# Tree attention on one core: loads in groups of four heads by first use, transposes behind the values and two pairs ahead

## The chip, the cores and the metric

The kernel runs on one core of one Trainium2 chip. The metric is device time in microseconds for one execution. The core's engines are TensorE (PE in the profile, with its weight loads as PEld), VectorE (DVE), ScalarE (ACT), GpSimd (POOL) and SyncE (SP), and 16 DMA engines move data.

## What is computed

Attention for 8 batches of 12 heads, with 512 positions of 64 elements each, in float32. The positions are the nodes of a binary tree, and each attends to itself and to its ancestors alone.

```python
    scale = 1.0 / np.sqrt(dim)
    mask = np.zeros((seq, seq))
    for i in range(seq):
        mask[i, i] = 1
        parent = i
        while parent > 0:
            parent = (parent - 1) // 2
            mask[i, parent] = 1

    scores = np.einsum('bhqd,bhkd->bhqk', Q, K) * scale
    scores = scores + (1 - mask) * (-1e9)
    weights = np.exp(scores - np.max(scores, axis=-1, keepdims=True))
    weights = weights / (np.sum(weights, axis=-1, keepdims=True) + 1e-10)
    return np.einsum('bhqk,bhkd->bhqd', weights, V).astype(np.float32)
```

## The kernel before

**Units.** The work unit is a pair of heads: 8 batches of 6 pairs, 48 pairs, numbered 0 to 47. A head's 512 positions lie as 128 partitions of 4 positions each. The mask is not added as numbers: two small constant matrices of codes (`ctile`) multiplied with each other give a large negative number where a query must not see a key, and TensorE accumulates q times k onto it in PSUM. Because each node has few ancestors, only two strips of scores are made, `st` (one key tile for all queries) and `stx` (for each of four groups of queries its own key tile), instead of the full 512 by 512.

**Loads.** `load` (L216) issues DMAs from GpSimd that read float32 from HBM and write bf16 tiles `qs`, `ks`, `vs`, one tile per batch and kind, six buffers of each. The list `plan` (L200) holds (iteration from which it may be issued, tensor, batch, first head, last head), and it is worked off in its written order: in batches 1 to 6 mostly Q and K of heads 0 to 5, V of the next batch, then Q and K of heads 6 to 11. Nothing but `load` runs on GpSimd. A load waits for the load eight before it, whose semaphore it takes over.

**A pair's steps.**
- `transposes(i)`: TensorE turns q and k of two heads by 16 matmuls into the PSUM tiles `tq` and `tk`; VectorE copies `tq` to `qt` (L297), ScalarE copies `tk` to `kt` (L298). q and k must have landed.
- `scores(i)`: into `st` two mask matmuls and two of q and k, then ScalarE's exponential to `et` (L324); into `stx` two mask matmuls and eight of q and k, then the exponential to `etx` (L335).
- `values(i)`: 24 matmuls of `et` and `etx` with V in the layouts `v1` and `vx`, whose last column of ones gives the sum of the weights, into the PSUM tile `o`; VectorE takes the reciprocal of the sums (`rec`, L364) and multiplies (`of`, L367); SyncE issues the output DMA (L371).
- `spread(b)` makes the layouts `v1` and `vx` of a batch from `vs`, as ten copies on VectorE (L261), three buffers of each layout.

Each of the PSUM tiles `tq`, `tk`, `st`, `stx`, `o` has one buffer.

**Order.** TensorE, VectorE, ScalarE and GpSimd each execute in the written order. The prologue is `load(3)`, `transposes(0)`, `scores(0)`, `transposes(1)`, the spread of six heads of batch 0, `transposes(2)`. Then iteration i issues:

```python
            load(i + 9)
            if i + 1 < N:
                scores(i + 1)
            if i + 3 < N:
                transposes(i + 3)
            values(i)
```

and after it one or two copies of the next batch's spread. So q and k of a pair are transposed two iterations before the iteration whose scores read them.

Of the kernel before, what the change touches and what calls it, by code (L numbers as in the profile page):

```python
# [126 lines left out]
def kernel(  # L127
# [8 lines left out]
    B, H, S, D = Q.shape  # L136
# [3 lines left out]
    HP = H // 2  # L140
# [11 lines left out]
    for t in range(T):  # L152
        o = sorted(range(T), key=lambda r: KCOL[t, r])
        at = [KCOL[t, r] for r in o]
# [32 lines left out]
    for i in range(NV):  # L187
# [10 lines left out]


    plan = [(0, Q, 0, 0, 2), (0, K, 0, 0, 2), (0, V, 0, 0, 6), (0, Q, 0, 2, 6),  # L200
            (0, K, 0, 2, 6), (0, V, 0, 6, H), (0, Q, 0, 6, H), (0, K, 0, 6, H),
            (3, Q, 1, 0, 6), (3, K, 1, 0, 6), (3, V, 1, 0, H), (6, Q, 1, 6, H),
            (6, K, 1, 6, H), (6, V, 2, 0, H)]
    for b in range(2, B):
        at = HP * b - 3
        plan += [(at, Q, b, 0, 6), (at, K, b, 0, 6)]
        if b < B - 1:
            plan += [(at + 2, V, b + 1, 0, H), (at + 3, Q, b, 6, H),
                     (at + 3, K, b, 6, H)]
        else:  # L210
            plan += [(at + 3, Q, b, 6, 10), (at + 3, K, b, 6, 10),
                     (at + 5, Q, b, 10, H), (at + 5, K, b, 10, H)]
    plan.reverse()
    loaded = {}
# [1 line left out]
    def load(upto):  # L216
        while plan and plan[-1][0] <= upto:
            _, src, b, h0, h1 = plan.pop()
            kind = "q" if src is Q else "k" if src is K else "v"
            if (kind, b) not in loaded:  # L220
                loaded[kind, b] = stage.tile([P, H, T * D], bf16, name=kind + "s")
            nc.gpsimd.dma_start(  # L222
                out=loaded[kind, b][:, h0:h1, :],
                in_=src[b, h0:h1].rearrange("h (p t) d -> p h (t d)", t=T),
            )
# [33 lines left out]
    def copies(ops):  # L259
        for o, i in ops:  # L260
            nc.vector.tensor_copy(out=o, in_=i)  # L261

    pairs = [(b, hp) for b in range(B) for hp in range(HP)]
    N = len(pairs)
    state = {}

    def transposes(i):
        b, hp = pairs[i]
        qs, ks = loaded["q", b], loaded["k", b]
        tq = psumT.tile([P, 512], bf16)  # L270
        tk = psumT.tile([P, 576], bf16)

        def put(o, src, t, mat):
            for hi in range(2):
                nc.tensor.matmul(  # L275
                    out=o[D * hi:D * hi + D], rhs=perms[mat],
                    lhsT=src[:, 2 * hp + hi, D * t:D * t + D],
                    start=True, stop=True, is_transpose=True,
                )

        put(tq[:, 64:192], qs, 0, 1)
        put(tq[:, 0:384].rearrange("d (c x) -> d c x", c=2)[:, :, 0:64], qs, 1, 0)
        for t in range(2, T):
            put(tq[:, P * t:P * t + P], qs, t, 0)
        for t in range(T):
            at = kput[t][1]
            if at[1] - at[0] == 32:
                step, run = at[2] - at[0], 64
            else:
                step, run = at[1] - at[0], 32  # L290
                assert at[2] - at[1] == step
            o = tk[:, at[0]:]
            o = bass.AP(o.tensor, o.offset, [list(o.ap[0]), [step, P // run], [1, run]])
            put(o, ks, t, 2 + t)
        qt = work.tile([P, 512], bf16)
        kt = work.tile([P, 512], bf16)
        nc.vector.tensor_copy(out=qt[:, :], in_=tq[:, :])  # L297
        nc.scalar.copy(  # L298
            out=kt[:, :].rearrange("d (i j x) -> d i j x", j=2, x=32),
            in_=tk[:, :].rearrange("d (j i x) -> d i j x", j=2, x=32)[:, 0:8],  # L300
        )
        state[i] = (qt, kt)

    def scores(i):
        b, hp = pairs[i]
        q_, k_ = state[i]
        st1 = psumS.tile([P, 2, 512], fp32)
        stx = psumS.tile([P, 2, 512], fp32)

        def mm(dst, lhsT, rhs, first):  # L310
            nc.tensor.matmul(  # L311
                out=dst, lhsT=lhsT, rhs=rhs, start=first, stop=True,
                skip_group_check=not first,
            )

        hb = [slice(D * hi, D * hi + D) for hi in range(2)]
        q = [q_[hb[hi], :] for hi in range(2)]
        k = [k_[hb[hi], :] for hi in range(2)]
        for hi in range(2):
            mm(st1[:, hi, :], ck1[hb[hi], :], cq1[hb[hi], :], True)  # L320
        for hi in range(2):
            mm(st1[:, hi, :], k[hi][:, 32 * K1:32 * K1 + P], q[hi], False)
        et1 = et1pool.tile([P, 2, 512], bf16)
        nc.scalar.activation(  # L324
            out=et1[:, :, :], in_=st1[:, :, :], func=AF.Exp, scale=scale
        )
        for hi in range(2):
            mm(stx[:, hi, 0:384], ckx[hb[hi], :], cqx[hb[hi], :], True)
        for c in range(T):
            for hi in range(2):  # L330
                mm(stx[:, hi, 96 * c:96 * c + 96],
                   k[hi][:, 32 * XW[c]:32 * XW[c] + P],
                   q[hi][:, P * c + 32:P * c + P], False)
        etx = etxs[i % NX]
        nc.scalar.activation(  # L335
            out=etx[:, :, :, 32:P],
            in_=stx[:, :, 0:384].rearrange("p h (c q) -> p h c q", c=T),
            func=AF.Exp, scale=scale,
        )
        state[i] = (et1, etx)  # L340

    def values(i):
        b, hp = pairs[i]
        v1, vx = v1s[b % NV], vxs[b % NV]
        et1, etx = state.pop(i)
        o2 = psumO.tile([P, 2, 512], fp32)
        for hi, order in ((0, (0, 1)), (1, (0, 1)), (0, (2, 3)), (1, (2, 3))):
            h = 2 * hp + hi
            for t in order:
                for kind in range(2):  # L350
                    parts = ((0, P, t),) if t >= 2 else (
                        (0, 64, 1 - t), (64, P, t))
                    for p0, p1, c in parts:
                        if kind == 0:
                            e, v = et1[:, hi, P * c + p0:P * c + p1], v1[:, h, 0:D + 1]
                        else:
                            e, v = etx[:, hi, c, p0:p1], vx[:, h, c, 0:D + 1]
                        nc.tensor.matmul(  # L358
                            out=o2[p0:p1, hi, (D + 1) * t:(D + 1) * (t + 1)],
                            lhsT=e, rhs=v, start=kind == 0, stop=kind == 1,  # L360
                        )
        o4 = o2[:, :, 0:T * (D + 1)].rearrange("p h (t x) -> p h t x", t=T)
        rec = opool.tile([P, 2, T, 1], fp32)
        nc.vector.reciprocal(out=rec[:, :, :, :], in_=o4[:, :, :, D:D + 1])  # L364
        of = opool.tile([P, 2, T * D], fp32)
        of4 = of[:, :, :].rearrange("p h (t d) -> p h t d", t=T)
        nc.vector.tensor_tensor(  # L367
            out=of4, in0=o4[:, :, :, 0:D],
            in1=rec[:, :, :, :].to_broadcast([P, 2, T, D]), op=ALU.mult,
        )  # L370
        nc.sync.dma_start(  # L371
            out=out[b, 2 * hp:2 * hp + 2].rearrange(
                "h (p t) d -> p h (t d)", t=T
            ),
            in_=of[:, :, :],
        )

    E = mybir.EngineType
    with tc.manual_schedule(engines={E.PE, E.DVE, E.Activation, E.Pool}):
        load(3)  # L380
        transposes(0)
        scores(0)
        transposes(1)
        copies(spread(0, 0, 6))
        transposes(2)
        for i in range(N):
            b, hp = pairs[i]
            load(i + 9)
            if i + 1 < N:
                scores(i + 1)  # L390
            if i + 3 < N:
                transposes(i + 3)
            values(i)
            if b == 0:
                if hp in (0, 3):
                    todo = spread(0, 6, H) if hp == 0 else spread(1, 0, H)
                cuts = (0, 3, 6, 10)
                copies(todo[cuts[hp % 3]:cuts[hp % 3 + 1]])
            elif b + 1 < B:
                if hp == 0:  # L400
                    todo = spread(b + 1, 0, H)
                cuts = (0, 1, 3, 5, 6, 8, 10)
                copies(todo[cuts[hp]:cuts[hp + 1]])


# [28 lines left out]
```

## Time and profile before

| | us |
|---|---|
| median of 13 executions | 158.77 (157.67 to 161.07) |
| the profiled execution, device time | 161.07 |
| its span, first to last instruction | 159.0 |
| TensorE matmuls busy | 116.8 (73%) |
| ScalarE busy | 105.8 (67%) |
| VectorE busy | 103.4 (65%) |
| GpSimd busy | 38.5 (24%) |
| load queue (q0), share of 16 DMA engines | 87.8% |
| output queue (q1), share of 16 DMA engines | 28.6% |
| mean granted TensorE clock | 0.931 |

The span is what the profile covers; the device time of the same execution has about 2 us more around it. The shares of the two DMA queues are the times that their packets took, and packets of both queues overlap on an engine, so their sum can pass 100%. TensorE's clock is granted in stretches: it is 1.00 or 0.50 of full speed. Busy shares are means over the whole span; the span has a long stretch in which the DMA engines are full and a shorter one at the end in which they are not.

### The profile page before, as it was taken

To read this page: it belongs to the slowest core of one execution; us is meant where nothing else is said; L and a number is where in the kernel's file an instruction comes from. 1 tells how busy PE (TensorE), PEld (TensorE's weight loads), DVE (VectorE), ACT (ScalarE), POOL (GpSimd) and SP (SyncE) were. 2 spreads that over 40 slices of the span, in tenths; PEclk is the share of its full clock that TensorE was granted. 3 is DMA by queue.
4 is the path that set the end of the run, shared out by engine and by line. 5 is a ranking of instruction groups with operands and counts; after the bars stand their busy time and mean duration, and the time that the engine had idled before them with its cause. 6 is when DMAs were issued, how large, how long until landed. Compare 5 with 4: busy or idle time off the path is not lost.

```text
span 159.0 us, 5902 instructions
## 1 busy us (share of the span) xinstructions
PE 116.8 (73%) x2592; PEld 85.4 (54%) x2592; DVE 103.4 (65%) x243; ACT 105.8 (67%) x145; POOL 38.5 (24%) x49
## 2 busy tenths in 40 slices
PE   0437599683999169995999189987977179998960
PEld 0215377462767047773777157756754058776740
DVE  2107567898999315994799437995979125996541
ACT  3142467685899317995699448986978117998950
POOL 7955441331321224222222224221301000000000
PEclk9999999999999957999599969999999956999998
DMA  5999999999999999999999999999999998442342
GB/s 140 147 181 197 197 199 220 222 232 233 220 235 236 239 221 199 229 235 244 221 229 236 243 221 220 221 241 236 226 237 233 241 197 157 139 138 95 122 154 99
DMA packets 50953, 32.32 MB, mean 203 GB/s; under 512 B 1520, under 2 KB 50800, under 8 KB 50928
## 3 DMA queue, kind: packets, MB, share of 16 engines
q0 software_dynamic: 37584, 18.88, 87.8%
q1 hardware_dynamic: 13344, 13.08, 28.6%
q8 instruction: 20, 0.33, 0.8%
q14 instruction: 5, 0.04, 0.1%
HBM read 38.24 MB, written 12.58 MB: 320 GB/s over the span
## 4 chain that ended last, share of the span: by engine, by line
DMA 76%; PE 8%; DVE 5%; issue 3%; POOL 3%; ACT 2%; ACTq 0%; POOLq 0%
DMA qs<-in_Q_dram 40%; DMA ks<-in_K_dram 36%; PE o L358 3%; DVE of L367 2%; PE st L311 2%; ACT etx L335 2%; PE stx L311 1%; DVE vx L261 1%; POOL vs L222 1%; POOL qs L222 1%; PE tk L275 1%; POOL ks L222 1%; PE tq L275 1%; DVE rec L364 1%; ACT et L324 1%
## 5 line engine op out<-in xcount | busy, mean ns | idle before, releaser
L324 ACT ACTIVATE et<-st 128x1024 bf16<-128x1024 f32 x48 | 50.5, 1053 | 19.6 <-PE st L311 19.5
L298 ACT COPY kt<-tk 128x512 bf16<-128x512 bf16 x48 | 29.6, 616 | 26.7 <-PE tk L275 26.7
L358 PE MATMUL o<-v,et 128*64 128x65 bf16 (+1 forms) x576 | 38.9, 204 | 6.6 <-DVE v L261 4.0
L335 ACT ACTIVATE etx<-stx 128x768 bf16<-128x768 f32 x48 | 40.1, 836 | 0.4 <-PE stx L311 0.4
L358 PE MATMUL o<-vx,etx 128*64 128x65 bf16 (+1 forms) x576 | 38.6, 202 | 0.0
L358 PEld LDWEIGHTS <-et 128*64 128x64 bf16 (+1 forms) x576 | 31.0, 113 | 9.0 <-DVE v L261 4.5
L367 DVE TENSOR_TENSOR of<-o,rec 128x512 f32<-128x512 f32 x48 | 33.2, 691 | 1.8 <-DVE rec L364 0.2
L275 PE MATMUL tq<-ptile,qs 128*64 128x128 bf16 x384 | 21.9, 242 | 14.9 <-DMA qs<-in_Q_dram 13.3
L275 PE MATMUL tk<-ptile,ks 128*64 128x128 bf16 x384 | 21.6, 241 | 14.9 <-DMA ks<-in_K_dram 14.6
L297 DVE COPY qt<-tq 128x512 bf16<-128x512 bf16 x48 | 20.2, 422 | 18.2 <-PE tq L275 17.2
L358 PEld LDWEIGHTS <-etx 128*64 128x64 bf16 (+1 forms) x576 | 30.9, 114 | 1.2 <-issue 1.2
L261 DVE COPY vx<-vs 32x1536 bf16<-32x1536 bf16 (+3 forms) x54 | 28.4, 526 | 1.5
L364 DVE RECIPROCAL rec<-o 128x8 f32<-128x8 f32 x48 | 9.7, 202 | 29.4 <-PE o L358 29.2
L311 PEld LDWEIGHTS <-kt 64*128 64x128 bf16 x480 | 20.4, 100 | 9.2 <-issue 4.6
L275 PEld LDWEIGHTS <-ks 128*64 128x64 bf16 x384 | 15.4, 123 | 16.5 <-DMA ks<-in_K_dram 16.2
L275 PEld LDWEIGHTS <-qs 128*64 128x64 bf16 x384 | 13.9, 118 | 19.0 <-DMA qs<-in_Q_dram 14.7
L222 POOL DMA_DIRECT2D qs<-in_Q_dram x18 | 15.1, 841 | 35.0 <-DMA qs<-in_Q_dram 10.5
L222 POOL DMA_DIRECT2D ks<-in_K_dram x18 | 14.7, 819 | 31.6 <-DMA vs<-in_V_dram 10.2
L311 PE MATMUL st<-qt,kt 64*128 64x512 bf16 x96 | 20.4, 413 | 0.2
L311 PE MATMUL st<-ctile 64*128 64x512 bf16 x96 | 20.4, 420 | 0.0
L311 PEld LDWEIGHTS <-ctile 64*128 64x128 bf16 x192 | 12.2, 97 | 14.1 <-issue 5.1
L311 PE MATMUL stx<-qt,kt 64*128 64x96 bf16 x384 | 18.4, 213 | 1.0 <-issue 1.0
(11 smaller groups left out, 42.8 us busy)
## 6 DMA issues: line engine op xcount, KB each, us to landing
out_dram<-of SPq DMA_DIRECT2D x48, 256.0 KB, 6.3
qs<-in_Q_dram POOLq DMA_DIRECT2D x14, 384.0 KB, 27.5
ks<-in_K_dram POOLq DMA_DIRECT2D x14, 384.0 KB, 26.4
vs<-in_V_dram POOLq DMA_DIRECT2D x7, 768.0 KB, 27.2
vs<-in_V_dram POOLq DMA_DIRECT2D x2, 384.0 KB, 9.0
qs<-in_Q_dram POOLq DMA_DIRECT2D x2, 256.0 KB, 16.6
ks<-in_K_dram POOLq DMA_DIRECT2D x2, 256.0 KB, 16.0
ctile<-tree_codes SPq DMA_DIRECT2D x1, 288.0 KB, 2.8
```

The costliest lines, as they stand in the source:

```text
L222: nc.gpsimd.dma_start(out=loaded[kind, b][:, h0:h1, :], in_=src[b, h0:h1].rearrange("h (p t) d -> p h (t d)", t=T),)
L261: nc.vector.tensor_copy(out=o, in_=i)
L275: nc.tensor.matmul(out=o[D * hi:D * hi + D], rhs=perms[mat], lhsT=src[:, 2 * hp + hi, D * t:D * t + D], start=True, stop=True, is_transpos ...
L297: nc.vector.tensor_copy(out=qt[:, :], in_=tq[:, :])
L298: nc.scalar.copy(out=kt[:, :].rearrange("d (i j x) -> d i j x", j=2, x=32), in_=tk[:, :].rearrange("d (j i x) -> d i j x", j=2, x=32)[:, 0:8],
L311: nc.tensor.matmul(out=dst, lhsT=lhsT, rhs=rhs, start=first, stop=True, skip_group_check=not first,)
L324: nc.scalar.activation(out=et1[:, :, :], in_=st1[:, :, :], func=AF.Exp, scale=scale)
L335: nc.scalar.activation(out=etx[:, :, :, 32:P], in_=stx[:, :, 0:384].rearrange("p h (c q) -> p h c q", c=T), func=AF.Exp, scale=scale,)
L358: nc.tensor.matmul(out=o2[p0:p1, hi, (D + 1) * t:(D + 1) * (t + 1)], lhsT=e, rhs=v, start=kind == 0, stop=kind == 1,)
L364: nc.vector.reciprocal(out=rec[:, :, :, :], in_=o4[:, :, :, D:D + 1])
L367: nc.vector.tensor_tensor(out=of4, in0=o4[:, :, :, 0:D], in1=rec[:, :, :, :].to_broadcast([P, 2, T, D]), op=ALU.mult,)
```

## The change

It has three parts.

1. The load plan. From batch 1 on, Q and K come in three groups of four heads instead of two of six, each group placed in the order in which its pairs are used, with V of the next batch between the second and the third group; batch 0 is split in the same manner. There are 61 load instructions instead of 45, for the same bytes.
2. The iteration's order on TensorE. It was scores(i+1), transposes(i+3), values(i). It becomes scores(i+1), values(i), transposes(i+2), and `transposes(2)` leaves the prologue. On VectorE the copy `qt` therefore stands behind `rec` and `of` of the iteration instead of ahead of them.
3. The spread copies of the next batch. In batches 1 to 6 they start with the second pair of the batch instead of the first, and come two at a time.

```diff
     plan = [(0, Q, 0, 0, 2), (0, K, 0, 0, 2), (0, V, 0, 0, 6), (0, Q, 0, 2, 6),
-            (0, K, 0, 2, 6), (0, V, 0, 6, H), (0, Q, 0, 6, H), (0, K, 0, 6, H),
-            (3, Q, 1, 0, 6), (3, K, 1, 0, 6), (3, V, 1, 0, H), (6, Q, 1, 6, H),
-            (6, K, 1, 6, H), (6, V, 2, 0, H)]
-    for b in range(2, B):
-        at = HP * b - 3
-        plan += [(at, Q, b, 0, 6), (at, K, b, 0, 6)]
+            (0, K, 0, 2, 6), (0, V, 0, 6, H), (1, Q, 0, 6, 10), (1, K, 0, 6, 10),
+            (3, Q, 0, 10, H), (3, K, 0, 10, H), (3, V, 1, 0, H)]
+    for b in range(1, B):
+        at = HP * b - 2
+        plan += [(at, Q, b, 0, 4), (at, K, b, 0, 4),
+                 (at + 2, Q, b, 4, 8), (at + 2, K, b, 4, 8)]
         if b < B - 1:
-            plan += [(at + 2, V, b + 1, 0, H), (at + 3, Q, b, 6, H),
-                     (at + 3, K, b, 6, H)]
+            plan += [(at + 3, V, b + 1, 0, H), (at + 4, Q, b, 8, H),
+                     (at + 4, K, b, 8, H)]
         else:
-            plan += [(at + 3, Q, b, 6, 10), (at + 3, K, b, 6, 10),
+            plan += [(at + 4, Q, b, 8, 10), (at + 4, K, b, 8, 10),
                      (at + 5, Q, b, 10, H), (at + 5, K, b, 10, H)]
...
         copies(spread(0, 0, 6))
-        transposes(2)
         for i in range(N):
             b, hp = pairs[i]
             load(i + 9)
             if i + 1 < N:
                 scores(i + 1)
-            if i + 3 < N:
-                transposes(i + 3)
             values(i)
+            if i + 2 < N:
+                transposes(i + 2)
             if b == 0:
                 if hp in (0, 3):
                     todo = spread(0, 6, H) if hp == 0 else spread(1, 0, H)
                 cuts = (0, 3, 6, 10)
                 copies(todo[cuts[hp % 3]:cuts[hp % 3 + 1]])
-            elif b + 1 < B:
-                if hp == 0:
+            elif b + 1 < B and hp:
+                if hp == 1:
                     todo = spread(b + 1, 0, H)
-                cuts = (0, 1, 3, 5, 6, 8, 10)
-                copies(todo[cuts[hp]:cuts[hp + 1]])
+                copies(todo[2 * hp - 2:2 * hp])
```

## The prediction

> **What bounds the kernel now.** I read the page first, for the share of each resource; then the chain of waits, for what ended last; then the timeline of one pair of heads without a stall, for durations and latencies.
>
> ```profile
> span 159.0 us, 5902 instructions
> ...
> DMA  5999999999999999999999999999999998442342
> ...
> DMA 76%; PE 8%; DVE 5%; issue 3%; POOL 3%; ACT 2%; ACTq 0%; POOLq 0%
> ```
>
> Each digit of the DMA row is 4 us. The 16 DMA engines are full up to about 133 us and a third busy in the last 26. So there are two stages: one in which transfers set the pace, and a tail in which compute works off what is left. The chain shows where one becomes the other:
>
> ```profile
> 97.11 31.09 DMA ks<-in_K_dram
> 128.20 0.04 issue
> 128.25 0.64 PE tk L275 x8
> ...
> 154.91 0.69 DVE of L367
> ```
>
> At 128.2 TensorE gets the second half of K of batch 6, for the transposes of pair 39. The values of pair 36 stand behind them, so pairs 36 to 47, twelve of 48, come after 128.2: the next `of` (one per pair) starts at 130.16, the twelfth at 154.91. That is 24.75 us for 11 steps, 2.25 us each. The last load was issued at 121.05 and took 16.0 us, so it landed at 137.06.
>
> Now one pair at the full clock, from the timeline (start, duration; a line with xN holds N instructions):
>
> ```profile
> 144.66 0.19 PE L358 MATMUL o<-vx,etx 128*128 128x65 bf16 x1
> ...
> 144.89 0.21 DVE L364 RECIPROCAL rec<-o 128x8 f32<-128x8 f32 x1 [0.55 <-PE o L358]
> 145.01 0.38 PE L311 MATMUL st<-qt,kt 64*128 64x512 bf16 x2
> 145.13 0.69 DVE L367 TENSOR_TENSOR of<-o,rec 128x512 f32<-128x512 f32 x1
> ...
> 145.49 1.02 ACT L324 ACTIVATE et<-st 128x1024 bf16<-128x1024 f32 x1 [0.62 <-PE st L311]
> 145.65 0.41 PE L275 MATMUL tq<-ptile,qs 128*64 128x128 bf16 x8
> ...
> 145.90 0.39 PE L275 MATMUL tk<-ptile,ks 128*64 128x128 bf16 x8
> 146.11 0.42 DVE L297 COPY qt<-tq 128x512 bf16<-128x512 bf16 x1 [0.29 <-PE tq L275]
> 146.12 0.20 PE L358 MATMUL o<-v,et 128*64 128x65 bf16 x2
> ...
> 147.05 0.38 PE L311 MATMUL st<-qt,kt 64*128 64x512 bf16 x2
> 147.10 0.59 ACT L298 COPY kt<-tk 128x512 bf16<-128x512 bf16 x1
> ```
>
> TensorE repeats after 147.05 - 145.01 = 2.04 us and has no gap. The scores at 147.05 use q and k copied well before; the copy `qt` at 146.11 is for a pair two iterations on. This slack is what the change touches. How soon TensorE follows a copy is seen at the start, where it has nothing else to do:
>
> ```profile
> 7.33 0.58 ACT L298 COPY kt<-tk 128x512 bf16<-128x512 bf16 x1 [5.32 <-PE tk L275]
> ...
> 7.97 0.61 PE L311 MATMUL st<-qt,kt 64*128 64x512 bf16 x2
> ```
>
> The copy ends at 7.91, the matmul starts at 7.97: 0.06 us.
>
> **What the Trainium skill says.** "TensorE: Matmul & The Clock Gate", section "Step-by-step: what each phase is for": matmuls stay in program order, only weight loads are pulled ahead. The trace agrees: between 124.56 (tq of pair 39) and 128.25 (its tk, waiting for K) no matmul of the values behind it runs. The same page, section "What's actually happening": the clock is halved until a window of about 3.4 us was busy, and falls back after an idle one. The trace agrees: the granted clock is 0.50 from 126.8 to 133.7, after the wait, and a pair's values take 0.99 us there and 0.60 after; from 24.43 to 55.15 it is 1.00 with PE busy 22.98 of 30.72 us, 75%. "DMA: Bandwidth & Descriptors", section "Issuing engines are not separate DMA queues": transfers from all engines run on the same 16 DMA engines and interleave. The trace agrees: once outputs flow, the loads slow down (below).
>
> **The change part by part.**
>
> *Loads.* Bytes are the same. Sixteen more DMA issues (61 load instructions against 45) at about 0.82 us on POOL are 13 us more of POOL, which is busy 38.5 us of 159 and has nothing else: hidden. POOL holds eight loads in flight (the issue at 10.90 waits for the third load, landed at 10.62); eight loads of four heads are still many packets for each DMA engine, so I take no loss of rate. What changes is when a pair's data is there. Before, 252 heads (a head of Q, K or V) landed from 19.24 to 137.06, 0.467 us each, with outputs between. A batch is 36 heads, 16.8 us, 2.80 us a pair. With as many outputs as loads in flight it is nearer 2.85: three pairs of 42 more, at 0.91 us (queue 1 took 28.6% of 159 us for 13.08 MB, of which a pair's output is 1/50). So loads need about 2.85 us a pair whatever the order, and end near 137.06 + 6 x 0.91 = 142.5 if the outputs keep up.
>
> *Slack removed on TensorE.* After the change one iteration is scores(i+1), values(i), transposes(i+2), and the next begins with scores(i+2). DVE's order is rec(i), of(i), qt(i+2), then spread copies; ACT's is et, etx, kt, as before. So scores need q and k of the transposes just ahead of them, and on DVE q's copy stands behind the normalisation of the values. Call S the start of the first st matmul that reads q and k; at the full clock:
> - S to the values: 0.64 (145.01 to 145.65, the place of tq before).
> - Values to their last matmul 0.58 (146.12 to 146.70), from it to rec 0.23 (144.66 to 144.89): rec at S + 1.45.
> - of 0.24 later (145.13 - 144.89): S + 1.69. The next DVE instruction follows of by 0.72 (142.37 to 143.09): qt at S + 2.41. Its source is ready by then: tq starts at S + 1.34 and ends at S + 1.75.
> - qt takes 0.42, plus 0.06 to TensorE: next S at S + 2.89. With 0.03 for seams, 2.92 us a pair.
> The other way round, through ACT: et starts 0.48 after S, etx 0.92 later, kt 0.69 after that (146.41 to 147.10) at S + 2.09, ends at S + 2.68, TensorE at S + 2.74. So DVE is last, by 0.15 us, and if it were faster ACT would hold 2.74. TensorE's own work is 2.04; only the two mask matmuls of st can run ahead, so about 0.9 us of each pair becomes a wait. Spread copies of at most 1.14 us (two of 0.57) run after qt and end before the next rec: hidden. In batch 0 one step has four (1.88 us): 0.3 us once.
>
> *Starving.* At 2.92 us a pair against 2.85 for loads, loads should stay ahead. Pair 10, the third group of batch 1, needs 84 heads: 19.24 + 48 x 0.467 = 41.7 us, used at 43.4 (S(9) + 1.34, by the sum below). Later margins grow slowly. The copies that read V of the next batch block DVE until V lands; V3 (112 heads, 54.7 us by the same rate) is used at about 59. No stall, but margins of 2 to 5 us only.
>
> *Sum.* Start: K of heads 2 to 5 lands at 13.25; the first values wait for the ten spread copies, which end at 17.23 in the trace; transposes(2) follow, and S(2) is at 20.2 (before: 21.25). The clock is still halved: by the same steps with the values of 0.99 us and the other slow durations one pair takes about 4 us, S(3) = 24.3. Then the full clock: S(4) = 27.2, S(47) = 27.2 + 43 x 2.92 + 0.3 = 153.1. After S(47): values(47) wait for of(46) to free the one PSUM tile, S + 2.5; of(47) starts 1.07 after its values do (153.84 to 154.91) and ends at S + 4.3; from there to the end 3.4 (155.6 to 159.0). Span 153.1 + 7.7 = 160.8. The profiled execution took 161.07 for a span of 159.0, so 2.07 lies around it: **162.9 us**. That execution was the slowest of the 13 shown, 2.3 above the median 158.77. I don't scale by this: the new sum rests on latencies, not on the loads' luck.
>
> **Rivals.**
> 1. *The latency loop sets the pace* (66%): 162.9; a loop of 2.80 to 3.00 us gives 43 x -0.12 = -5.2 and 43 x 0.08 = +3.4, so 157.7 to 166.3.
> 2. *The loads set the pace* (14%, the other side: faster). Strict order lets each pair run as its data lands, and the tail of twelve pairs shrinks to two. For it: DMA is full to 133 us, and in the 22 us after the last landing the DMA engines are two thirds idle. Last load at 142.5, about 1.3 to S(47), 7.7 to the end: 151.5 + 2.1 = 153.6. It decides as soon as the loop is clearly below 2.85 us, for instance if the modelled matmul ends are late and DVE starts sooner. Against it: the steps above are starts of DVE and ACT instructions, which are measured.
> 3. *A tie* (8%): the loop falls at about 2.83, near the loads' pace; 159.
> 4. *More is lost* (12%). TensorE at 75% could fall back to half clock: fifteen pairs at 1 us more, 178. Or the thin margins break and V's wait on DVE adds to the loop: a microsecond or two per batch, 168. Against the clock: it held at 75% above.
>
> **How the numbers follow.** The likeliest case gives 162.9. The range 156.5 to 167.5 holds case 1, the tie and the mild half of case 4; below it lies case 2, above it the lost clock. A measurement here tells about 0.5% from no change (158.0 to 159.6). Faster 0.14 (case 2), same 0.09 (the tie and the edge of case 1), slower 0.77.
>
> **What would show it.** Right: starts of `of` about 2.9 us apart from 30 us to the end; TensorE waiting about 0.8 us in each pair, at st, for DVE's qt; almost no wait of transposes for DMA; the last load landing near 142 with five or so pairs left to do. Wrong: transposes still waiting for qs and ks after 60 us (case 2), `of` 2.7 us apart or less, or long stretches of clock 0.5 (case 4).

## The result and the profile after

| | before | after |
|---|---|---|
| median device time, us | 159.01 (48 executions, 156.89 to 161.26) | 160.41 (11 executions, 158.56 to 162.09) |
| span of the profiled execution, us | 159.0 | 158.1 |
| device time of the profiled execution, us | 161.07 | 159.86 |

The change makes the kernel 1.1% slower: the ratio of after to before is 1.0111, with a 95% interval of 1.0077 to 1.0145. A ratio, here and below, takes from each kernel only the executions within 1.5% of its fastest, so it is not the quotient of the medians. The two profiled executions stand the other way round, because the one of before was among its longest and the one of after in the lower half of its own. So spans of single profiles are not set against each other below; steps within a profile are.

The page of the kernel after, with the rows that answer to those of before:

```profile
PEclk9999999999999999999999999999999999999996
DMA  5999999999999999999999999999999999823222
...
DVE 45%; PE 42%; DMA 5%; issue 4%; POOL 1%; ACT 1%; POOLq 0%
```

The DMA row still looks full, and a glance at it would say that nothing has changed. The chain of waits says otherwise: 76% of it were DMA before, and now 87% are VectorE and TensorE in turn. TensorE's clock is full from 22.4 us, where its record begins, to 155.5. Before 22.4 us TensorE is slow, which the row does not show: the two matmuls of st take 0.60 us at 18.70, and 0.39 in the loop. In the profile of before the clock was at half for 20.5 us in four stretches, each behind a wait for loads.

The waits of after (who waited for whom; total, times, longest):

```profile
PE st L311 <- DVE qt L297: 20.8, 44, 0.9
...
PE tq L275 <- DMA qs<-in_Q_dram: 7.7, 2, 5.8
...
PE tk L275 <- DMA ks<-in_K_dram: 0.7, 1, 0.7
```

The same rows before:

```profile
PE tk L275 <- DMA ks<-in_K_dram: 14.6, 7, 3.3
PE tq L275 <- DMA qs<-in_Q_dram: 13.3, 5, 6.0
```

The transposes wait for q only twice and for k once, where before they waited twelve times and 28 us. Instead st waits for qt in 44 of 48 pairs. One pair of the timeline shows the loop:

```profile
44.88 0.39 PE L311 MATMUL st<-qt,kt 64*128 64x512 bf16 x2 [0.46 <-DVE qt L297]
...
45.53 0.22 PE L358 MATMUL o<-v,et 128*64 128x65 bf16 x2
...
46.26 0.41 PE L275 MATMUL tq<-ptile,qs 128*64 128x128 bf16 x8
...
46.36 0.21 DVE L364 RECIPROCAL rec<-o 128x8 f32<-128x8 f32 x1 [0.59 <-PE o L358]
...
46.60 0.69 DVE L367 TENSOR_TENSOR of<-o,rec 128x512 f32<-128x512 f32 x1
...
46.98 0.59 ACT L298 COPY kt<-tk 128x512 bf16<-128x512 bf16 x1
47.21 0.41 DVE L297 COPY qt<-tq 128x512 bf16<-128x512 bf16 x1
...
47.68 0.39 PE L311 MATMUL st<-qt,kt 64*128 64x512 bf16 x2 [0.46 <-DVE qt L297]
```

Follow the starts: st 44.88, values 45.53, rec 46.36, of 46.60, qt 47.21, next st 47.68. That is a step of 2.80 us, and most steps from pair 9 on are 2.80 within 0.01. tq, issued at 46.26, is done by 46.67, half a microsecond before qt: the data is there, but qt's turn on VectorE is not. ScalarE's copy kt ends at 47.57, only 0.05 us ahead of qt at 47.62, so a second path is almost as long.

At the turn of a batch a step is longer. Pair 12 is the first of batch 2:

```profile
52.81 0.41 DVE L297 COPY qt<-tq 128x512 bf16<-128x512 bf16 x1
53.26 0.55 DVE L261 COPY vx<-vs 32x1536 bf16<-32x1536 bf16 x1
53.82 0.45 DVE L261 COPY v<-vs 32x768 bf16<-32x768 bf16 x1
```

```profile
54.32 0.22 PE L358 MATMUL o<-v,et 128*64 128x65 bf16 x2 [0.32 <-DVE v L261]
```

In the first of these two stretches VectorE writes the last two copies of batch 2's layouts; in the second TensorE's values(12) wait for the last of them and start 0.39 us later than in a 2.80 us step. The step is 3.19. Six turns of this kind cost 3.09 to 3.19 instead of 2.80. In batch 0 the same wait is larger: steps of 3.56 (pair 5) and 4.12 us (pair 8). One more long step, 3.24 us at pair 6, is of another kind: rec itself stands behind three copies there and starts at 31.04, when the last of them ends at 31.01.

### The profile page after: what moved, and what is told of

It is laid out like the page before. It is cut to its first block, busy times and chain, and to the rows that moved or that the text cites. A ratio compares the mean times of both kernels' runs of the same rounds, so it can differ in the third digit from the quotient of the medians.

```text
span 158.1 us, 5916 instructions
## 1 busy us (share of the span) xinstructions
PE 118.3 (75%) x2592; PEld 83.2 (53%) x2592; DVE 102.4 (65%) x243; ACT 108.3 (69%) x145; POOL 48.8 (31%) x65
## 4 chain that ended last, share of the span: by engine, by line
DVE 45%; PE 42%; DMA 5%; issue 4%; POOL 1%; ACT 1%; POOLq 0%
PE o L358 23%; DVE of L367 20%; DVE qt L297 10%; PE st L311 9%; PE stx L311 8%; DVE rec L364 6%; DVE vx L261 5%; DMA qs<-in_Q_dram 5%; DVE v L261 3%; PE tq L275 1%; ACT kt L298 1%; PE tk L275 1%; POOL qs L222 1%; POOL vs L222 1%; POOL ks L222 0%
## 5 line engine op out<-in xcount | busy, mean ns | idle before, releaser
L324 ACT ACTIVATE et<-st 128x1024 bf16<-128x1024 f32 x48 | 49.1, 1023 | 29.8 <-PE st L311 29.8
L311 PEld LDWEIGHTS <-kt 64*128 64x128 bf16 x480 | 22.5, 96 | 42.1 <-ACT kt L298 33.3
L358 PE MATMUL o<-v,et 128*64 128x65 bf16 (+1 forms) x576 | 37.3, 201 | 5.5 <-DVE v L261 4.4
L358 PE MATMUL o<-vx,etx 128*64 128x65 bf16 (+1 forms) x576 | 36.3, 196 | 0.0
L311 PE MATMUL st<-qt,kt 64*128 64x512 bf16 x96 | 19.5, 394 | 21.4 <-DVE qt L297 20.8
L364 DVE RECIPROCAL rec<-o 128x8 f32<-128x8 f32 x48 | 9.9, 207 | 38.4 <-PE o L358 38.1
L358 PEld LDWEIGHTS <-et 128*64 128x64 bf16 (+1 forms) x576 | 27.9, 107 | 11.9 <-DVE v L261 4.7
L222 POOL DMA_DIRECT2D qs<-in_Q_dram x26 | 20.3, 782 | 44.0 <-DMA vs<-in_V_dram 28.5
L358 PEld LDWEIGHTS <-etx 128*64 128x64 bf16 (+1 forms) x576 | 28.7, 108 | 0.0
L222 POOL DMA_DIRECT2D ks<-in_K_dram x26 | 19.4, 746 | 27.1 <-DMA qs<-in_Q_dram 17.8
L275 PE MATMUL tq<-ptile,qs 128*64 128x128 bf16 x384 | 20.8, 232 | 7.7 <-DMA qs<-in_Q_dram 7.7
L275 PE MATMUL tk<-ptile,ks 128*64 128x128 bf16 x384 | 19.7, 227 | 0.8 <-DMA ks<-in_K_dram 0.7
L275 PEld LDWEIGHTS <-qs 128*64 128x64 bf16 x384 | 12.7, 113 | 10.5 <-DMA qs<-in_Q_dram 7.9
L311 PE MATMUL stx<-ctile 64*128 64x384 bf16 x96 | 16.9, 334 | 0.0
```

Source lines behind the costliest of these rows:

```text
L222: nc.gpsimd.dma_start(out=loaded[kind, b][:, h0:h1, :], in_=src[b, h0:h1].rearrange("h (p t) d -> p h (t d)", t=T),)
L275: nc.tensor.matmul(out=o[D * hi:D * hi + D], rhs=perms[mat], lhsT=src[:, 2 * hp + hi, D * t:D * t + D], start=True, stop=True, is_transpos ...
L311: nc.tensor.matmul(out=dst, lhsT=lhsT, rhs=rhs, start=first, stop=True, skip_group_check=not first,)
L324: nc.scalar.activation(out=et1[:, :, :], in_=st1[:, :, :], func=AF.Exp, scale=scale)
L358: nc.tensor.matmul(out=o2[p0:p1, hi, (D + 1) * t:(D + 1) * (t + 1)], lhsT=e, rhs=v, start=kind == 0, stop=kind == 1,)
```

## The experiments

Each is the changed kernel with one edit, unless it says otherwise. "Ratio" is to the kernel before, timed beside it, with its 95% interval; times are medians of all executions.

**Loads alone.** The kernel before with the new load plan, order and copies as before (+ and - against the kernel before):

```diff
-            (3, Q, 1, 0, 6), (3, K, 1, 0, 6), (3, V, 1, 0, H), (6, Q, 1, 6, H),
...
+        plan += [(at, Q, b, 0, 4), (at, K, b, 0, 4),
+                 (at + 2, Q, b, 4, 8), (at + 2, K, b, 4, 8)]
...
```

> The kernel before with one edit: the load plan of the changed kernel (groups of four heads by first use); TensorE keeps scores, transposes three ahead, values. Theory A (the order made the loss, the load plan is a gain that it hides): the tail after the last landing shrinks from twelve pairs to about four, last load near 140, three more pairs at about 2.05 us and 7.7 us to the end: 154 to 157 us, ratio to before 0.97 to 0.99. Theory B (the sixteen further DMA issues and the smaller loads in flight cost, and the order is neutral): 160 to 161, as the changed kernel.

Measured: 157.24 us in four executions, ratio 0.9845 (0.9781 to 0.9909). The load plan by itself is a gain, of 1.1% by the medians (157.24 against 158.96) and 1.5% by the ratio. The time is 0.2 us above theory A's range; in the profiled execution the last load lands at 138.6 and 17.0 us follow, against 22 before, so the tail shrinks, though by less than was expected. Theory B falls: 61 smaller loads cost no time that shows, though the last one lands 1.5 us later than before (137.1).

**Order alone.** The changed kernel with the load plan of before:

```diff
-            (0, K, 0, 2, 6), (0, V, 0, 6, H), (1, Q, 0, 6, 10), (1, K, 0, 6, 10),
+            (0, K, 0, 2, 6), (0, V, 0, 6, H), (0, Q, 0, 6, H), (0, K, 0, 6, H),
...
```

> The changed kernel with one edit: the load plan of the kernel before (groups of six heads, V between). Theory A: the loop through VectorE holds 2.80 us a pair from about 25 us on, and K of heads 6 to 11 of batch 6, which landed at 128.2 before, comes about 1.5 us after its pair would use it: 161 to 163 us, ratio 1.015 to 1.03. Theory B: without the small loads the loss is gone, 158 to 159.5.

Measured: 161.4 us, ratio 1.0150 (1.0119 to 1.0181), with the same steps of 2.80 us. The time is in theory A's range, but one of its reasons did not come about: K of heads 6 to 11 of batch 6 landed at 127.33 and its transposes took it at 127.71 without a wait. The order with its copies costs 1.5% where the loads stay as they were. The order makes the loss, and the plan cannot repay it, because behind this order the loads are no longer what is waited for.

**Reciprocal twice.** A sensitivity test of the loop: the reciprocal of every pair is computed a second time.

```diff
         nc.vector.reciprocal(out=rec[:, :, :, :], in_=o4[:, :, :, D:D + 1])
+        nc.vector.reciprocal(out=rec[:, :, :, :], in_=o4[:, :, :, D:D + 1])
```

> The changed kernel with one instruction doubled: the reciprocal of each pair is computed twice in a row (0.21 us busy, about 0.24 from start to start). If rec, of and qt on VectorE are the loop, every pair pays it in full: steps of 3.04 instead of 2.80 us, 47 x 0.24 = 11 us more, span about 169. If the loads, ScalarE or TensorE set the pace, VectorE (busy 65%) hides it: span 158 to 160.

Measured in one execution: 172.33 us, span 170.6, steps of 3.04 us. Two stretches of VectorE's timeline in it, one pair apart:

```profile
46.13 0.21 DVE L364 RECIPROCAL rec<-o 128x8 f32<-128x8 f32 x1 [0.38 <-PE o L358]
46.38 0.21 DVE L365 RECIPROCAL rec<-o 128x8 f32<-128x8 f32 x1
...
49.17 0.21 DVE L364 RECIPROCAL rec<-o 128x8 f32<-128x8 f32 x1 [0.59 <-PE o L358]
```

The two reciprocals start 0.25 apart and the next pair's rec comes 3.04 after this one's, 0.24 more than in the kernel after: an engine that is busy 65% of the span passes the addition on in every pair, because it lies on the loop. The span is 1.6 us above the 169 expected. Of the 12.5 us that it is longer than after, 10.4 lie in the 43 steps after pair 4, the rest at the start and the end.

**Transposes first, still two ahead.** TensorE does scores(i+1), transposes(i+2), values(i):

```diff
-            values(i)
             if i + 2 < N:
                 transposes(i + 2)
+            values(i)
```

> The changed kernel with one edit: TensorE does scores(i+1), transposes(i+2), values(i), so the lead stays two pairs and only the places of values and transposes are swapped; on VectorE qt stands ahead of rec and of again. If VectorE's order alone made the loop, it falls to the next path, which is ScalarE's (et 0.49 after S, etx 0.92, kt 0.69 later, kt 0.59, 0.06 to TensorE): 2.74 to 2.76 us a pair where no load is awaited, and 154 to 158 us in all. If the lead of two pairs doesn't matter once qt is early, the steps fall to 2.05 to 2.16 us, as with three pairs ahead. If the place behind the values was not the cause, steps stay at 2.80 and the time at 160.4.

Measured: 158.8 us, ratio 1.0007 (0.9982 to 1.0033), just above the range given. The step is exactly the expected 2.75. ScalarE's timeline, and TensorE's after it:

```profile
109.56 1.02 ACT L324 ACTIVATE et<-st 128x1024 bf16<-128x1024 f32 x1 [0.55 <-PE st L311]
110.48 0.81 ACT L335 ACTIVATE etx<-stx 128x768 bf16<-128x768 f32 x1
111.17 0.59 ACT L298 COPY kt<-tk 128x512 bf16<-128x512 bf16 x1
```

```profile
109.06 0.39 PE L311 MATMUL st<-qt,kt 64*128 64x512 bf16 x2 [0.52 <-ACT kt L298]
...
111.81 0.39 PE L311 MATMUL st<-qt,kt 64*128 64x512 bf16 x2 [0.54 <-ACT kt L298]
```

st now waits for kt, the copy on ScalarE behind et and etx, as worked out before the run. So VectorE's order was the first limit, but by 0.05 us only: with a lead of two pairs scores stand right behind the transposes' copies, and ScalarE's path holds 2.75. The time misses its range because at 2.75 the loads begin to be awaited: the 43 steps after pair 4 sum to 126.5 us instead of 43 x 2.75 = 118.3, and the long ones are where pairs 8 to 10, 16, 22 and 28 to 30 stand. At most of these (10, 16, 22, 28) tk waits for K, at pair 8 the values wait 1.79 us for a layout copy, and the clock is at half from 36.3 to 39.7 (pair 9) and from 94.3 to 101.2 us (pairs 28 and 29).

**Three ahead.** The transposes stay behind the values, but are those of pair i+3:

```diff
         copies(spread(0, 0, 6))
+        transposes(2)
...
-            if i + 2 < N:
-                transposes(i + 2)
+            if i + 3 < N:
+                transposes(i + 3)
```

> The changed kernel with one edit: the transposes, still behind the values, are of pair i+3 instead of i+2 (pair 2 in the prologue again). Theory A: q and k then have a whole iteration for their copies, the loop falls to TensorE's and ScalarE's 2.04 to 2.07 us, the loads set the pace, TensorE waits for q and k landings, and few pairs are left at the end: last load near 141, S of pair 47 about 4 later, 7.7 to the end: 153 to 156 us, ratio 0.96 to 0.98. Theory B (the load plan or the shorter lead itself costs): 159 to 161.

Measured: 157.09 us in four executions, ratio 0.9832 (0.9761 to 0.9903), a microsecond above the range. ScalarE runs without a gap, at 2.16 us a pair where nothing is awaited, not at the 2.04 to 2.07 expected:

```profile
62.04 1.02 ACT L324 ACTIVATE et<-st 128x1024 bf16<-128x1024 f32 x1
62.96 0.81 ACT L335 ACTIVATE etx<-stx 128x768 bf16<-128x768 f32 x1
63.65 0.59 ACT L298 COPY kt<-tk 128x512 bf16<-128x512 bf16 x1
64.20 1.02 ACT L324 ACTIVATE et<-st 128x1024 bf16<-128x1024 f32 x1
```

So the place behind the values does not by itself cost 2.80: with a lead of three the same place gives 2.16, and 157.09 us cannot be told from the 157.24 of the loads alone. The transposes' tq and tk wait 20.8 us for q and k again: the loads set the pace. The last load lands at 140.1 in the profiled execution (issued at 127.4, 12.7 to landing) and 13.6 us follow, against 22 before. I had 12 (4 to the last pair's scores and 7.7 from there). K of pairs 40 to 47 landed from 127.10 to 140.14, 1.86 us a pair and so faster than 2.16, and the transposes of pair 47 start 3.1 us after their K landed. From there to its scores another 2.6 us pass, in which the scores of pair 46 come first: this is the lead itself.

**Copies earlier.** The spread copies go with pairs 0 to 4 of a batch instead of 1 to 5:

```diff
-            elif b + 1 < B and hp:
-                if hp == 1:
+            elif b + 1 < B and hp < 5:
+                if hp == 0:
                     todo = spread(b + 1, 0, H)
-                copies(todo[2 * hp - 2:2 * hp])
+                copies(todo[2 * hp:2 * hp + 2])
```

> The changed kernel with one edit: the spread copies of the next batch go with pairs 0 to 4 of a batch instead of 1 to 5. If the first values of a batch wait for the last copies of its spread (the steps of 3.1 to 3.2 us instead of 2.80, one in six, from batch 2 on), six steps lose 0.3 to 0.4 us each: 158 to 158.7 us, 1.9 less than the changed kernel's 160.4, and all steps from pair 14 on are 2.80. If these steps come from something else at the turn of a batch (the first use of a newly loaded tile), no change: 160.4. A loss, 161 or more, would show that V of the next batch is then awaited on VectorE.

Measured: 158.77 us, ratio 1.0005 (0.9975 to 1.0036), 1.6 below the changed kernel. The row of the waits that was 4.4 us and 9 times in the kernel after is here

```profile
PE o L358 <- DVE v L261: 2.6, 3, 1.1
```

so six of nine waits of the values for a copy are gone, and all steps of pairs 9 to 26 are 2.80 or 2.81. The turns of the batches were this wait. The time is just above the range, and not all later steps are 2.80: those of pairs 27, 30, 33 and 39 are 2.96 to 3.23. At three of these the first copy of a batch, with rec behind it, waits for V:

```profile
DVE vx L261 <- DMA vs<-in_V_dram: 1.7, 3, 0.7
```

There was no such wait in the kernel after. The landings fit this: in the profile after, the loads of batches 1 to 7 land from 18.34 to 138.65, 2.86 us for each of 42 pairs (2.89 in this run). Its steps with the long ones were 2.90 on average, a little slower than the loads; 2.80 is faster.

**All copies earlier.** In addition batch 0's copies are spread anew:

```diff
-                if hp in (0, 3):
+                if hp in (0, 2):
...
-                cuts = (0, 3, 6, 10)
-                copies(todo[cuts[hp % 3]:cuts[hp % 3 + 1]])
+                cuts = ((0, 5), (5, 10), (0, 2), (2, 5), (5, 8), (8, 10))
+                copies(todo[slice(*cuts[hp])])
```

> The changed kernel with the spread copies of batches 1 to 6 one pair earlier and, in batch 0, its second half in two steps (pairs 0 and 1) and batch 1's layout from pair 2 on (2, 3, 3, 2 copies). If the long steps of batch 0 (3.56 and 4.12 us instead of 2.80, at the pairs whose values are the first to use a finished layout) are the same wait as at the later turns, they fall to about 2.8 and 3.1: 0.7 and 1.0 us less than with the later batches alone (158.8), 156.8 to 157.5. If they come from the slow start (half clock, loads still scarce), no change: 158.8.

Measured: 158.72 us, ratio 1.0014 (0.9984 to 1.0043): no gain over the run above. In its profile the steps did fall as expected (pairs 5 to 7 at 2.80, pair 8 at 3.10), so these were the same wait. But the gain did not reach the end. The profiled execution, the longest of the 22, shows one way of losing it, on VectorE:

```profile
91.53 1.38 DVE L261 COPY vx<-vs 64x1536 bf16<-64x1536 bf16 x2 [2.69 <-DMA vs<-in_V_dram]
92.84 0.18 DVE L364 RECIPROCAL rec<-o 128x8 f32<-128x8 f32 x1
```

A layout copy waits 2.69 us for V of batch 5, and rec stands behind it; with three shorter ones these waits are 4.0 us. The execution profiled of the run above (158.17 us, in the usual range) had three of the same kind, and the loads land at 2.88 us a pair here too. That the usual executions of this version lose the gain in this way is likely from this, but not shown, as the profile is of the longest one.

**Three ahead with copies earlier.** Both versions of the copies on top of three ahead:

> The changed kernel with two edits: transposes three pairs ahead behind the values, and the spread copies with pairs 0 to 4 of a batch. Against three pairs ahead alone (157.1, steps of 3.1 to 3.3 us at the turn of each batch among steps of 2.16): if those turns cost in the stretches that no load paces, 0.5 to 1.5 us less, 155.5 to 156.6. If the loads take up what is gained, 157.1. If VectorE now waits for V of the next batch with rec queued behind it, 158 or more.

> Three pairs ahead behind the values, and all spread copies as early as in the run beside it. If the loads pace this version, as its waits for q and k landings say, nothing is gained over the 157.1 and 157.35 of three ahead before: 156.5 to 157.5. If its start counts, 155 to 156.5, and this is the version that beats both kernels by most.

Measured: 157.35 us, ratio 0.9813 (0.9738 to 0.9888), and 156.49 us, ratio 0.9865 (0.9809 to 0.9921). They rest on six executions each, the run with three ahead alone on four. The intervals of the three versions overlap, so the copies' place changes nothing here that can be told; that the loads take up what the turns give fits this, but is not shown. All three are faster than the kernel before, by 0.9 to 1.5% by the medians and 1.3 to 1.9% by the ratios, and so is the load plan alone; none was timed beside the changed kernel.

## Why the prediction was right or wrong

The loop that was forecast is there, but its step was put too large, and a wait that the forecast held hidden was not: 162.9 us, 2.6% above the 158.77 of before, were forecast, 160.41 and 1.1% came. Against the profiled execution, term by term:

| term | predicted | measured |
|---|---|---|
| S of pair 4 | 27.2 | 25.55 |
| 43 steps at the plain rate | 43 x 2.92 = 125.6 | 43 x 2.80 = 120.4 |
| longer steps | 0.3 | 4.5 |
| from the last S to the end | 7.7 | 7.7 |
| around the span | 2.07 | 1.76 |
| sum | 162.9 | 159.9 |

- *The step that failed: "The next DVE instruction follows of by 0.72".* This took qt behind of from the copy vx behind of. Measured, qt starts 0.61 after of, 0.08 us before of ends, in every pair of the loop. The trace of before had a nearer case in its rows:

```profile
139.56 0.42 DVE L297 COPY qt<-tq 128x512 bf16<-128x512 bf16 x1
139.90 0.20 DVE L364 RECIPROCAL rec<-o 128x8 f32<-128x8 f32 x1
...
142.37 0.69 DVE L367 TENSOR_TENSOR of<-o,rec 128x512 f32<-128x512 f32 x1
143.09 0.55 DVE L261 COPY vx<-vs 32x1536 bf16<-32x1536 bf16 x1
```

  There rec follows qt after 0.34 us although qt takes 0.42, also 0.08 early. The other parts of the loop: st to rec 1.48 (1.45 predicted), rec to of 0.24 (0.24), qt to st 0.47 (0.48). The 0.03 for seams was not there. Together 0.12 us a pair, 5.2 us in 43.
- *A second step that failed: "Spread copies ... run after qt and end before the next rec: hidden".* Hidden from rec, but for the step of pair 6 (0.44 us, where 0.3 was put down for batch 0); I did not ask who else waits for them. The values of a batch's first pair read the layout whose last copies stand behind qt in the iteration before. This cost 0.3 to 0.4 us at six turns (2.0 together) and 2.1 at two steps of batch 0; all long steps are 4.2 us over what I had put down. That the six turns are this wait is shown by the copies' earlier place, and the two of batch 0 by the run with all copies earlier.
- *The start* was 1.65 us too late, 1.5 of it already at S of pair 2 (18.70, not 20.2). K of heads 2 to 5 landed at 12.32 in this execution, not at 13.25, and the ten copies ahead of the first values ended at 15.76, not at 17.23. That landing varies from 11.71 to 13.61 over all profiles, so this is partly the execution's own start.
- *"I don't scale by this".* The reason given was that the sum rests on latencies, not on the loads' luck; the start did rest on that luck. The profiled execution of before was 2.3 us above the median of 158.77 that my sum was set against. Of its own kind, span to span, the sum said 1.1%; that it agrees with the measured ratio is chance, since the terms above erred by several microseconds in both directions.
- *That a loss came* is in part luck. The forecast's own sum for a loop of 2.80 gives 157.7, less than before. What makes 2.80 a loss is the wait at the turns, which it held hidden: with the six turns taken away the ratio is 1.0005.
- *The loads' end.* The pace of 2.85 us a pair was right (2.86), but the end of 142.5 doesn't follow from it: the pace counts the outputs of three more pairs, the end those of six. 42 pairs at 2.85 from 19.24 end at 138.9; the last load landed at 138.65. As the forecast said of loads behind outputs, a head took 0.33 us to land before the first output (12.32 to 15.64, ten heads) and 0.48 on average later.
- *Right:* st waits for qt, though 0.46 us on TensorE after its mask matmuls and not 0.8; from pair 2 on transposes no longer wait for loads; the last load landed with five pairs' scores still to do (pairs 43 to 47); and ScalarE's path as the next limit, predicted 2.74 and found at 2.75 when VectorE's was taken away. TensorE's clock held at full speed through the loop, against the case in which it would fall. TensorE need not be idle for the clock to fall: in the profile of before a stretch of 3.41 us with matmuls in 47% of it (72.2 to 75.6) was followed by half clock, one with 52% (34.7 to 38.1) was not; the emptiest such stretch of the loop after, 36.1 to 39.5, has 55%.
- *The rival on the faster side* is real but needs another order: with three ahead the loads do set the pace, and 157 came instead of the 153.6 worked out for it, as 5.6 us and not 1.3 pass from the last landing to the last pair's scores.

## What to carry to other kernels

When a consumer is moved right behind its producer on one engine, walk once around the loop through the other engines, and put down for each where the copy between them stands in that engine's own order: here a lead of two pairs instead of three turned a step of 2.04 to 2.16 us into 2.80 while every engine stayed at 75% busy or less. The copy's place behind the normalisation is only 0.05 of it, since with the copy ahead of it the step was 2.75. Take each start-to-start time from a pair of the same two operations, or at least of the same kind, since 0.1 us is multiplied by the number of steps. For work that is called hidden, list all who wait for it, not only the instruction behind it.

## What the runs showed that was not expected

VectorE can begin an instruction before the one ahead of it has ended. It does so by 0.08 us in of to qt (46 of 46 in the profile after) and mostly in qt to rec (23 of the 25 that follow at once in the profile of before). In these cases both instructions read PSUM, but that is not what decides: in before, qt also starts 0.07 us before the end of a layout copy, which reads SBUF, in 7 of 7 cases where this copy writes from partition 0, as qt does, and 0.03 us or more after the end in all 31 where it writes from another partition (the order of the copies in `spread` gives the partitions). From of to a layout copy it is 0.03 us after the end, also in the 14 that write from partition 0, but these read from another. From rec to of it is 0.03 after as well; there the second needs the first's result. The lines under *All copies earlier* show rec 0.07 us before the end of a copy of the first kind. So in these profiles the early start goes with writing from the same partition on as the instruction ahead, though that is not enough, and with not needing its result. No run changed this alone.
